# Low parts of weights, masked queries and branch additions move from GpSimd to VectorE, and the planner lets the two engines exclude each other

## The chip, the cores and the metric

The kernel runs on one core of a Trainium2 chip. The core has five engines that run side by side, each with its own queue and its instructions in a fixed order: TensorE (in the profile PE for matmuls, PEld for the loading of weights), VectorE (DVE), ScalarE (ACT), GpSimd (POOL) and SyncE (SP), which issues most transfers. An engine stops at an instruction whose inputs are not there, and everything behind it in its queue stops too. The metric is the device time of one execution in microseconds (us); lower is better.

## What is computed

A batch of one, 512 tokens, 1024 features, all in float32. The first block has two layers. A layer normalizes the tokens (with 16 meta tokens in front, 528 in all), projects them with one wide matrix, runs four token mixers beside each other (A: attention in a window, B: attention with rotary positions, C: differential attention, D: a gated linear recurrence in both directions), gates and adds their results, and ends with a feed-forward network:

```python
for l in range(DEPTH):                                   # 2
    u = rms_norm(h, ln_mix[l])
    (aq, ak, av, bq, bk, bv, cq, ck, cv, dq, dzf, dzb, di, dg, gz) = split_in(u @ w_in[l])
    ...
    gate = jax.nn.sigmoid(gz).reshape(Bn, L, N_BRANCH, D_MODEL)
    merged = gate[:, :, 0] * (y_a @ w_branch[l, 0])
    for n, y in enumerate((y_b, y_c, y_d), start=1):
        merged = merged + gate[:, :, n] * (y @ w_branch[l, n])
    h = h + merged @ w_out[l]
    u = rms_norm(h, ln_ffn[l])
    h = h + (jax.nn.silu(u @ w_ffn_gate[l]) * (u @ w_ffn_up[l])) @ w_ffn_down[l]
```

The second block is one layer: a feed-forward network, a mixer (window attention beside an S5 state-space model) and a second feed-forward network, each with a norm before and after and with shifts and gains from a conditioning vector.

## The kernel before, in words

*Products in three parts.* Every large product runs as three fast matmuls (`mm3`, L258 to L260): a weight `w` and an activation `x` are each split into a high part, which the fast format holds exactly, and a low part, the rest, and high x high, low x high and high x low are added up in PSUM. So each piece of weight that comes from memory (`wload`, L191) goes through two engines: ScalarE copies it into the high part (L218), and a second engine subtracts that from the raw piece to get the low part (L219, pieces of 128x512, some of 128x256). Which engine does it says the list `lo_engs`: the weights of a list of two alternate between its engines. It is VectorE alone at the start, in the output projection (L1696) and in the gate and up projections of the first block's feed-forward networks; it is GpSimd and VectorE by turns in the token mixing of each layer (L1669) and from the start of a layer's down projection (L2186) on, which in the second layer holds for the whole second block. Activations are split likewise (`split`, L230 and L231), with their own choice of engine.

*Token mixing.* A layer first weaves the projections with branches A, B and C; then comes a stage with branch D (`branch_D`, four heads, `d_head`) woven with the merges of branches 1, 2 and 0, and behind it the merge of branch 3. For each head, D goes through levels of 32, 16, 8, 4, 2 and 1 tokens (L1407). A level takes a difference of running sums `d` (L1414, VectorE), its exponentials (L1416 and L1417, ScalarE), the keys times them `kt` (L1419, VectorE), and for levels of 16 and under the queries masked to one half of each block (`masked_q`, L1487, GpSimd), times the exponentials `qm` (L1434, VectorE). Then 16 small matmuls make the level's products on the diagonal blocks (L1403), and VectorE puts them in place by a mask (L1439). Per layer there are 4 x 5 = 20 masked queries.

*Merging.* For a branch `n` and each of eight blocks of features (`merge`, L1492) the kernel makes the gate from the wide projection (24 matmuls per half, tanh on ScalarE, L1514), multiplies it on VectorE with the branch's projection (12 matmuls, L1518), and from the second branch on adds that to the sum (L1520, GpSimd). Layer 0 does so in two halves of 272 and 256 columns, layer 1 in one of 512.

*Order.* Nothing of this is the order on the chip. The whole program is recorded, and then a planner (`Plan`, L2616) simulates it: each instruction has a price by its engine and size (`price`, L2797), there are prices for the signal from one engine to another, and a priority from the length of the work that hangs on it. At each step the engine that is free first takes the ready instruction of the highest priority (`run`, L2875). The order that comes out is written down as the order of every engine's queue, SP's with its transfers too. In the plan, VectorE and GpSimd don't know of each other: a VectorE instruction that is no copy costs 68 + n/0.96 ns for n columns, one of GpSimd 150 + 2.1 n, and after each the engine is free again 60 ns later. Between small matmuls that lie beside each other in the array there is a lower price (`beside`, L2767), and the shape in which the array is used costs nothing to change.

Of the kernel before, what the change touches and what calls it, by code (L numbers as in the profile page):

```python
# [17 lines left out]
ALU = mybir.AluOpType  # L18
PSUM = bass.MemoryType.PSUM
# [100 lines left out]
class Net:  # L120
# [1360 lines left out]
    def masked_q(self, q, m, c0, pool):  # L1481
        qm = self.act_tile(pool, "qm", 3)
        n2 = 2 * m
        o, w = self.offs["qmask"]
        mk = self.misc[:, o + QOFF[m]:o + QOFF[m] + n2]
        nb = (NT - c0) // n2
        self.nc.gpsimd.tensor_tensor(out=qm[:, c0:].rearrange("p (i s) -> p i s", s=n2), in0=q[:, c0:].rearrange("p (i s) -> p i s", s=n2),  # L1487
                                     in1=mk[:, None, :].to_broadcast([P, nb, n2]), op=ALU.mult)
        return qm


    def merge(self, l, n, y, merged, c0, first, pool):  # L1492
# [10 lines left out]
        for f in range(KC):  # L1503
# [13 lines left out]
            def ev2(ps, a, b):  # L1517
                V.scalar_tensor_tensor(out=(m if first else gt)[:, a:b], in0=gt[:, a:b], scalar=1.0, in1=ps, op0=ALU.add, op1=ALU.mult)  # L1518
                if not first:
                    nc.gpsimd.tensor_tensor(out=m[:, a:b], in0=m[:, a:b], in1=gt[:, a:b], op=ALU.add)  # L1520
# [119 lines left out]
    def block1(self, taps=None):  # L1640
        nc = self.nc
        taps = taps or {}
        for l in range(2):
# [10 lines left out]
            with self.pool(f"mix{l}") as mix:  # L1654
# [13 lines left out]
                with self.pool(f"att{l}", "R") as att, self.psum(mm="m"):  # L1668
                    self.lo_engs = [nc.gpsimd, nc.vector]  # L1669
# [141 lines left out]
class Net2(Net):  # L1811
# [368 lines left out]
    def hooks(self, l):  # L2180
# [3 lines left out]
        def down(f):  # L2184
            if f == 0:
                self.lo_engs = [self.nc.gpsimd, self.nc.vector]  # L2186
                if l == 0:
                    self.prep, self.late = self.ssm_prep(), []
                self.prep_on = True
# [426 lines left out]
class Plan:  # L2616
# [8 lines left out]
    TABLE_LOAD, QUEUE, LANES, LANE, DMA_END, DMA_START, WINDOW, WARM = 1283, 32, 8, 900, 940, 650, 3413, 3060  # L2625
# [53 lines left out]
    def trace(self):  # L2679
# [83 lines left out]
        for n, i in enumerate(self.ins):  # L2763
            if self.eng[n] == 0:
                place = self.columns_of(i)
                if place and last and place[0] == last[0] and not place[1] & last[1]:
                    self.beside[n] = last[2], int(2 + 51 * place[2] / 64) + 0  # L2767
# [6 lines left out]
    def written(self):  # L2774
        if not hasattr(self, "_written"):
            self._written = {x.bass_ap.tensor.name for i in self.nc.cur_bb.bb.instructions for x in i.outs if hasattr(x, "bass_ap")}
        return self._written

# [18 lines left out]
    def price(self, i, e, dma, aps):  # L2797
# [7 lines left out]
        if e == 0:  # L2805
# [4 lines left out]
            if mv.dtype == mybir.dt.float32r:  # L2810
                k = 4 if n < 256 else 1
                return int(max(n, m) * k / 2.4) + 3, n * k, 0
# [4 lines left out]
            return int(max(n, m) * 4 / 2.4) + 4, int(4 * n * part), 0  # L2817
# [57 lines left out]
    def run(self):  # L2875
        N = len(self.ins)
        self.columns, self.taken = defaultdict(float), {}
# [8 lines left out]
        free = [0] * 5  # L2886
        lanes, hw, bus, table = [], 0, 0, 0
# [41 lines left out]
        while count < total:  # L2929
# [48 lines left out]
            elif e == 0:  # L2978
                b = self.beside[n]
                c = (b[1] if b and b[0] == before else c[0]), c[1]  # L2980
                self.taken[n] = c[0]
                free[e] = end[n] = self.product(s, *c)
                before, follow = n, self.next.get(n)
            else:
# [4 lines left out]
                end[n] = s + c[0]  # L2989
# [60 lines left out]
```

## Time and profile before

| | us |
|---|---|
| median of three runs | 3429.25 |
| the runs | 3427.11, 3429.25, 3450.57 |
| the profiled execution | 3435.91 |
| its span, first to last instruction | 3434.0 |
| TensorE's mean granted clock in it | 0.939 of full |

The rows below come from the profiled execution. Times in the views count from the start of the span. "Busy" of TensorE counts time in which at least one matmul is under way; a row of matmuls gives each one's own duration, and these overlap. A wait row names the engine and line that waited, then the engine and line that released it, and the idle time, the number of waits and the longest. A stretch of the program stands at: 445 to 695 us branch D with merges in layer 0, 1490 to 1760 the same in layer 1, 150 to 445 and 1250 to 1490 the attention branches, 2150 to 2260 the down projection of layer 1 with the preparation of the S5 model beside it, 3060 to 3350 the last feed-forward network.

### The profile page before, as it was taken

Reading aid. Unit: us, or ns where it says so; the run is one execution under the profiler, and the core shown is the slowest. Engines: PE = TensorE matmul, PEld = TensorE weight load, DVE = VectorE, ACT = ScalarE, POOL = GpSimd, SP = SyncE. Lnnn points to the kernel's source line nnn. Section 1 sums busy time; section 2 is a strip of 40 time slices with the busy share of each in tenths; the row PEclk is TensorE's granted clock in tenths of the full one; section 3 lists DMA queues with packets and bytes.
Section 4 is the critical chain, followed back from the end, with each engine's and each line's share of the span. In section 5 each row is a group of like instructions: output and inputs, shape, how many; then the busy total and the mean of one; then the engine's idle time right before and its main releaser. Section 6 shows DMA issues by size and latency. Waiting matters only on the chain. (4 is left out here: it accounts for less than half of the span.)

```text
span 3434.0 us, 57894 instructions
## 1 busy us (share of the span) xinstructions
PE 3178.3 (93%) x21892; PEld 2775.5 (81%) x21892; DVE 1800.9 (52%) x4554; ACT 1278.3 (37%) x2856; POOL 1070.3 (31%) x952
## 2 busy tenths in 40 slices
PE   7888998999999988998889999999999999989997
PEld 6766877889999976876568888689888888888887
DVE  4556568745644957476875464754111633741113
ACT  2445443334232245653423322234333423542332
POOL 1212244432112331244452111653333411323333
PEclk9988999999999999999999999999999985989998
DMA  5621222344444672122234454474334542333343
GB/s 148 163 49 37 78 59 80 85 123 124 142 121 124 164 170 63 33 85 87 61 98 128 117 163 139 152 217 123 94 95 120 159 150 80 93 102 95 92 120 97
DMA packets 645885, 380.42 MB, mean 111 GB/s; under 512 B 66501, under 2 KB 613885, under 8 KB 645477
## 3 DMA queue, kind: packets, MB, share of 16 engines
q1 hardware_dynamic: 628520, 365.22, 36.5%
q0 software_dynamic: 13632, 9.61, 1.6%
q8 instruction: 172, 2.82, 0.3%
q10 hardware_dynamic: 3452, 1.89, 0.2%
q14 instruction: 109, 0.89, 0.1%
HBM read 333.16 MB, written 45.52 MB: 110 GB/s over the span
## 5 line engine op out<-in xcount | busy, mean ns | idle before, releaser
L258 PE MATMUL ps_mm<-u,wh 128*128 128x256 f32 (+2 forms) x2928 | 972.8, 333 | 38.6 <-ACT g L1514 10.1
L260 PE MATMUL ps_mm<-u,wh 128*128 128x256 f32 (+2 forms) x2928 | 962.5, 330 | 3.1 <-DVE u L231 3.1
L259 PE MATMUL ps_mm<-u,wh 128*128 128x256 f32 (+2 forms) x2912 | 956.2, 329 | 3.6 <-DVE wh L219 2.3
L258 PEld LDWEIGHTS ps_mm<-u,wh 128*128 128x128 f32 x2928 | 563.3, 193 | 100.7 <-ACT g L1514 13.2
L219 POOL TENSOR_TENSOR wh<-wr,wh 128x512 fp32r<-128x512 f32 (+1 forms) x280 | 374.1, 1349 | 764.0 <-ACT wh L218 542.6
L218 ACT ACTIVATE wh<-wr 128x512 fp32r<-128x512 f32 (+1 forms) x588 | 354.7, 618 | 686.5 <-PE ps_mm L260 285.9
L260 PEld LDWEIGHTS ps_mm<-u,wh 128*128 128x128 f32 x2928 | 561.8, 192 | 54.0 <-issue 4.5
L259 PEld LDWEIGHTS ps_mm<-u,wh 128*128 128x128 f32 x2912 | 559.9, 193 | 51.3 <-issue 3.4
L219 DVE TENSOR_TENSOR wh<-wr,wh 128x512 fp32r<-128x512 f32 (+1 forms) x251 | 184.5, 749 | 395.8 <-issue 120.2
L259 PE MATMUL ps_mm<-hid,wh 128*128 128x256 f32 (+2 forms) x988 | 301.9, 311 | 3.5 <-DVE wh L219 2.7
L258 PE MATMUL ps_mm<-hid,wh 128*128 128x256 f32 (+2 forms) x948 | 291.1, 313 | 0.0
L260 PE MATMUL ps_mm<-hid,wh 128*128 128x256 f32 (+2 forms) x948 | 290.9, 312 | 0.0
L231 POOL TENSOR_TENSOR hid<-g,hid 128x512 fp32r<-128x512 f32 (+1 forms) x85 | 93.1, 1096 | 518.5 <-ACT hid L230 513.4
L1846 DVE SCALAR_TENSOR_TENSOR acc<-ho,cact,acc 128x128 f32<-128x128 f32 x504 | 217.9, 438 | 27.6 <-DMA ho<-in_w_ada_dram 18.3
L259 PEld LDWEIGHTS ps_mm<-hid,wh 128*128 128x128 f32 x988 | 186.8, 191 | 14.8 <-DVE wh L219 3.6
L260 PEld LDWEIGHTS ps_mm<-hid,wh 128*128 128x128 f32 x948 | 179.4, 192 | 10.4 <-issue 0.8
L258 PEld LDWEIGHTS ps_mm<-hid,wh 128*128 128x128 f32 x948 | 179.5, 192 | 10.1 <-issue 0.4
L218 ACT ACTIVATE wh<-wrx 128x512 fp32r<-128x512 f32 (+1 forms) x160 | 96.1, 601 | 209.6 <-PE ps_mm L260 126.9
L258 PE MATMUL ps_mm<-u,hid 128*128 128x256 f32 (+1 forms) x448 | 136.7, 305 | 16.7 <-ACT hid L218 16.7
L259 PE MATMUL ps_mm<-u,hid 128*128 128x256 f32 (+1 forms) x448 | 136.4, 305 | 6.8 <-DVE hid L219 6.8
L219 DVE TENSOR_TENSOR wh<-wrx,wh 128x512 fp32r<-128x512 f32 x83 | 58.1, 700 | 150.8 <-issue 68.6
L260 PE MATMUL ps_mm<-u,hid 128*128 128x256 f32 (+1 forms) x448 | 134.8, 301 | 0.0
(599 smaller groups left out, 6152.2 us busy)
## 6 DMA issues: line engine op xcount, KB each, us to landing
wr<-in_w_in_dram SPq DMA_DIRECT2D x220, 256.0 KB
ho<-in_w_ada_dram SPq DMA_DIRECT2D x144, 256.0 KB
wr<-in_w_ffn_down_dram SPq DMA_DIRECT2D x80, 256.0 KB
wr<-in_w_down_dram SPq DMA_DIRECT2D x66, 256.0 KB
wr<-in_w_ffn_gate_dram SPq DMA_DIRECT2D x62, 256.0 KB
wr<-in_w_gate_dram SPq DMA_DIRECT2D x61, 256.0 KB
wr<-in_w_ffn_up_dram SPq DMA_DIRECT2D x60, 256.0 KB
wr<-in_w_up_dram SPq DMA_DIRECT2D x60, 256.0 KB
```

Source lines behind the costliest of these rows:

```text
L218: self.last_split = nc.scalar.activation(hi[:, i:e], raw, AF.Copy)
L219: (nc.vector if o else eng).tensor_tensor(out=lo[:, i:e], in0=raw, in1=hi[:, i:e].bitcast(F32), op=ALU.subtract)
L231: (eng or self.nc.vector).tensor_tensor(out=lo, in0=x, in1=hi.bitcast(F32), op=ALU.subtract)
L258: T.matmul(o, lhsT=wh, rhs=xh[:, a:b], start=start, stop=False)
L259: T.matmul(o, lhsT=wl, rhs=xh[:, a:b], start=False, stop=False)
L260: T.matmul(o, lhsT=wh, rhs=xl[:, a:b], start=False, stop=stop)
L1846: V.scalar_tensor_tensor(out=acc, in0=w[:, k], scalar=c, in1=acc, op0=ALU.mult, op1=ALU.add)
```

## The change

Four edits move work, and the rest changes the planner. All low parts are made on VectorE; the masked query of D and the addition of a branch go to VectorE as well. What stays on GpSimd: the low parts of activations that `split` gives it, the sums of squares, the copies into `U` at the start of a head of D, a few products of the S5 preparation and its DMA issues.

```diff
     def masked_q(self, q, m, c0, pool):
...
-        self.nc.gpsimd.tensor_tensor(out=qm[:, c0:].rearrange("p (i s) -> p i s", s=n2), in0=q[:, c0:].rearrange("p (i s) -> p i s", s=n2),
+        self.nc.vector.tensor_tensor(out=qm[:, c0:].rearrange("p (i s) -> p i s", s=n2), in0=q[:, c0:].rearrange("p (i s) -> p i s", s=n2),
...
                 if not first:
-                    nc.gpsimd.tensor_tensor(out=m[:, a:b], in0=m[:, a:b], in1=gt[:, a:b], op=ALU.add)
+                    V.tensor_tensor(out=m[:, a:b], in0=m[:, a:b], in1=gt[:, a:b], op=ALU.add)
...
                 with self.pool(f"att{l}", "R") as att, self.psum(mm="m"):
-                    self.lo_engs = [nc.gpsimd, nc.vector]
+                    self.lo_engs = [nc.vector]
...
         def down(f):
             if f == 0:
-                self.lo_engs = [self.nc.gpsimd, self.nc.vector]
+                self.lo_engs = [self.nc.vector]
```

In the planner, a VectorE instruction (engine 2 in the code) whose inputs all lie in SBUF, and a GpSimd instruction (engine 3) with more than one input, take a common "port": each begins when the port is free and holds it to its end. A change of the shape in which TensorE's array is used costs 95 or 190 ns, and some prices of matmuls change.

```diff
+    def shares(self, n, e):
+        if n not in self.sources:
+            aps = [x.bass_ap for x in self.ins[n].ins if getattr(x, "bass_ap", None) is not None]
+            psum = any(str(x.tensor.space).endswith("PSUM") for x in aps)
+            self.sources[n] = not psum and (e == 2 or e == 3 and len(aps) > 1)
+        return self.sources[n]
...
-                    self.beside[n] = last[2], int(2 + 51 * place[2] / 64) + 0
+                    self.beside[n] = last[2], int(2 + 8 * place[2] / 64)
...
-                k = 4 if n < 256 else 1
-                return int(max(n, m) * k / 2.4) + 3, n * k, 0
+                if n < 256:
+                    return max(105, int(n * 4 / 2.4)), n * 4, 0
+                return int(n * 0.449 + 3.5), n, 0
...
-            return int(max(n, m) * 4 / 2.4) + 4, int(4 * n * part), 0
+            return int(max(n, m) * 4 / 2.4) + 9, int(4 * n * part), 0
...
+                new = self.layout_of(n) or shape
+                if new != shape:
+                    c = c[0] + (self.REGROUP if new[0] == shape[0] else 2 * self.REGROUP), c[1]
+                    shape = new
...
-                end[n] = s + c[0]
+                begin = s
+                if self.shares(n, e):
+                    begin = max(s, port)
+                    port = begin + c[0]
+                end[n] = begin + c[0]
                 free[e] = end[n] + (20 if e == 1 else 60)
```

So the order of every engine is computed anew. VectorE in branch D of layer 0, head 0, levels 8 and 4, before (`d_`, `kt_` and `qm_` are a level's difference, keys and queries, `wb_` a low part, `hn_` the sum of branches):

```order
L1419 TENSOR_TENSOR kt_959_4719<-kk0_1573,d_958_4715 128x528
L1434 TENSOR_TENSOR qm_960_4721<-qm_960_4721,d_958_4715 128x528
L1518 SCALAR_TENSOR_TENSOR hn_1046_5228<-g_1047_5229,ps_mm_1051_5290 128x256
L1419 TENSOR_TENSOR kt_980_4850<-kk0_1573,d_979_4846 128x528
L1439 COPY_PREDICATED D_937_4573<-mask_484,ps_d_961_4724 128x128
L1434 TENSOR_TENSOR qm_981_4852<-qm_981_4852,d_979_4846 128x528
L219 TENSOR_TENSOR wb_1110_5645<-wr_1111_5646,wb_1110_5645 128x256
```

VectorE at the same place now (`wh_` is a low part of a weight of the wide projection):

```order
L1487 TENSOR_TENSOR qm_960_4721<-qq0_3992,misc_72 128x528
L1419 TENSOR_TENSOR kt_959_4719<-kk0_1573,d_958_4715 128x528
L1434 TENSOR_TENSOR qm_960_4721<-qm_960_4721,d_958_4715 128x528
L1487 TENSOR_TENSOR qm_981_4852<-qq0_3992,misc_72 128x528
L1414 TENSOR_TENSOR d_984_4876<-U_884_4294,lf0_3141 128x528
L219 TENSOR_TENSOR wb_1089_5499<-wr_1090_5500,wb_1089_5499 128x256
L1414 TENSOR_TENSOR d_1001_4991<-U_884_4294,lf0_3141 128x528
L219 TENSOR_TENSOR wh_1092_5505<-wr_1094_5510,wh_1091_5504 128x512
L1487 TENSOR_TENSOR qm_986_4882<-qq0_3992,misc_72 128x528
L1419 TENSOR_TENSOR kt_980_4850<-kk0_1573,d_979_4846 128x528
L1434 TENSOR_TENSOR qm_981_4852<-qm_981_4852,d_979_4846 128x528
```

Between two levels' queries (`qm_960` and `qm_981`) VectorE had three instructions, and now has seven: two masked queries, two low parts, two differences and the next keys.

GpSimd at that place, before:

```order
L219 TENSOR_TENSOR wh_1092_5505<-wr_1094_5510,wh_1091_5504 128x512
L1487 TENSOR_TENSOR qm_956_4694<-qq0_3992,misc_72 128x512
L1487 TENSOR_TENSOR qm_960_4721<-qq0_3992,misc_72 128x528
L219 TENSOR_TENSOR wh_1113_5651<-wr_1114_5652,wh_1112_5650 128x512
L1487 TENSOR_TENSOR qm_981_4852<-qq0_3992,misc_72 128x528
L1487 TENSOR_TENSOR qm_986_4882<-qq0_3992,misc_72 128x528
```

And now, where only the copies into `U` at the start of each head are left:

```order
L1309 COPY U_884_4294<-lf0_3141 64x528
L1315 COPY U_884_4294<-lf0_3141 64x8x63
L1313 MEMSET U_884_4294 64x8
L1314 COPY U_884_4294<-lf0_3141 64x15
L1310 MEMSET U_884_4294 64x1
L1309 COPY U_1028_5169<-lf0_3141 64x528
```

VectorE in the attention stretch of layer 1, at the first maxima of branch C (`ISA` on L1096), before:

```order
L219 TENSOR_TENSOR wh_2509_15243<-wr_2511_15248,wh_2508_15242 128x512
L1096 ISA g_2442_15010,tmC_2439_15007<-ps_s_2443_15011,tab_2437_15004 128x264
L1096 ISA tmC_2439_15007 128x1
L1096 ISA g_2442_15010,ngC_2440_15008<-ps_s_2444_15014,tab_2437_15004,tmC_2439_15007 128x264
L1096 ISA ngC_2440_15008 128x1
```

And now:

```order
L219 TENSOR_TENSOR wh_2509_15243<-wr_2511_15248,wh_2508_15242 128x512
L1096 ISA g_2442_15010,tmC_2439_15007<-ps_s_2443_15011,tab_2437_15004 128x264
L1096 ISA tmC_2439_15007 128x1
L219 TENSOR_TENSOR wh_2536_15354<-wr_2537_15355,wh_2535_15353 128x512
L1096 ISA g_2442_15010,ngC_2440_15008<-ps_s_2444_15014,tab_2437_15004,tmC_2439_15007 128x264
```

A low part that GpSimd made before stands between the two halves of a score row.

## Rows read from the trace of the kernel before

**Rows 1.** The page: busy us, share of the span and instructions by engine
```profile
PE 3178.3 (93%) x21892; PEld 2775.5 (81%) x21892; DVE 1800.9 (52%) x4554; ACT 1278.3 (37%) x2856; POOL 1070.3 (31%) x952
```
**Rows 2.** Stretches: start:end length, busy of PE, PEld, DVE, ACT, POOL, PEclk, DMA, GB/s
```profile
445.00:695.00 250.00, 228.86 (x2413) 198.11 (x2413) 195.94 (x381) 93.64 (x241) 120.16 (x103) 0.92 0.27 77
...
1250.00:1490.00 240.00, 213.66 (x1635) 176.00 (x1635) 144.35 (x591) 139.84 (x328) 51.99 (x45) 0.93 0.28 64
1490.00:1760.00 270.00, 234.52 (x1898) 171.24 (x1897) 206.53 (x329) 104.54 (x254) 127.65 (x102) 0.93 0.28 80
...
2150.00:2260.00 110.00, 103.19 (x548) 77.56 (x547) 85.68 (x111) 25.11 (x46) 77.09 (x49) 0.97 0.53 166
...
3060.00:3350.00 290.00, 290.00 (x1423) 242.85 (x1423) 45.98 (x75) 86.97 (x160) 95.45 (x79) 1.00 0.34 99
```
**Rows 3.** Waits of PE, first three from 450 to 700 us, then from 1500 to 1760
```profile
PE ps_mm L258 <- ACT g L1514: 8.4, 6, 3.7
PE ps_d L1403 <- DVE qm L1434: 7.1, 5, 2.6
PE ps_mm L258 <- DVE g L1518: 4.0, 3, 2.3
...
PE ps_mm L258 <- DVE hn L1518: 6.8, 3, 5.0
PE ps_mm L258 <- ACT g L1514: 6.6, 8, 2.0
PE ps_d L1403 <- DVE qm L1434: 5.7, 5, 2.3
PE ps_d L1463 <- DVE AO L1455: 4.0, 1, 4.0
PE ps_mm L258 <- DVE g L1518: 3.7, 3, 2.0
```
**Rows 4.** Timeline 511 to 516 us, start and length: GpSimd, VectorE, then TensorE
```profile
511.24 2.98 POOL L1487 TENSOR_TENSOR qm<-qq,misc 128x528 f32<-128x528 f32 x2
...
511.63 1.41 DVE L1419 TENSOR_TENSOR kt<-kk,d 128x528 f32<-128x528 f32 x1
512.97 1.81 DVE L1434 TENSOR_TENSOR qm<-qm,d 128x528 f32<-128x528 f32 x1
514.71 0.70 DVE L1419 TENSOR_TENSOR kt<-kk,d 128x528 f32<-128x528 f32 x1
...
514.84 0.46 PE L1403 MATMUL ps_d<-qm,kt 128*32 128x32 f32 x32 [1.76 <-DVE qm L1434]
```
**Rows 5.** Lines: busy us and mean ns, or duration ns min/median/max
```profile
L1434 DVE TENSOR_TENSOR qm<-qm,d 128x528 f32<-128x528 f32 (+1 forms) x40 | 48.9, 1223 | 0.0
L1419 DVE TENSOR_TENSOR kt<-kk,d 128x528 f32<-128x528 f32 (+1 forms) x48 | 56.5, 1177 | 19.0 <-PE ps_d L1380 9.0 <-PE ps_d L1391 4.5 <-PE ps_d L1427 2.7
...
L1434 DVE TENSOR_TENSOR qm<-qm,d x40: 677/1135/1943, 447.9 to 1735.9; 128x528 f32<-128x528 f32 x32, 128x512 f32<-128x512 f32 x8
...
L219 DVE TENSOR_TENSOR hid<-wr,hid x33: 676/680/1229, 809.0 to 3053.4; 128x512 fp32r<-128x512 f32 x33
...
L231 DVE TENSOR_TENSOR u<-g,u x56: 408/428/1506, 30.2 to 3055.9; 128x256 fp32r<-128x256 f32 x44, 128x272 fp32r<-128x272 f32 x12
```
**Rows 6.** Stretches, GpSimd's instructions of L219 alone: busy us and count, PEclk, DMA, GB/s
```profile
150.00:445.00 295.00, 39.23 (x30) 0.91 0.21 54
445.00:695.00 250.00, 54.33 (x40) 0.92 0.27 77
...
1250.00:1490.00 240.00, 24.47 (x19) 0.93 0.28 64
1490.00:1760.00 270.00, 69.12 (x49) 0.93 0.28 80
```
**Rows 7.** Waits of PE from 1250 to 1500 us
```profile
PE ps_s L1095 <- DVE tmC L1096: 10.4, 3, 4.8
```

More of the change, by code (lines that the diff above doesn't have):

```diff
@@ L2624 @@
     TABLES = {"Exp": 1, "Tanh": 1, "Sigmoid": 2, "Ln": 3, "Silu": 4}
-    TABLE_LOAD, QUEUE, LANES, LANE, DMA_END, DMA_START, WINDOW, WARM = 1283, 32, 8, 900, 940, 650, 3413, 3060
+    TABLE_LOAD, QUEUE, LANES, LANE, DMA_END, DMA_START, WINDOW, WARM, REGROUP = 1283, 32, 8, 900, 940, 650, 3413, 3060, 95
     def __init__(self, tc, slack):
@@ L2777, in written, with layout_of @@
         return self._written
+    def shares(self, n, e):
[4 more added lines that the diff above has]
+        return self.sources[n]
+    def layout_of(self, n):
+        if n not in self.layouts:
+            i = self.ins[n]
+            wt = i.ins[1].bass_ap if i.opcode == "Matmult" else None
+            self.layouts[n] = None if wt is None else tuple(next(s for s in (32, 64, 128) if x <= s) for x in (wt.ap[0][1], self.free(wt)))
+        return self.layouts[n]
     @staticmethod
@@ L2876, in run @@
         N = len(self.ins)
-        self.columns, self.taken = defaultdict(float), {}
+        self.columns, self.taken, self.layouts, self.sources, shape = defaultdict(float), {}, {}, {}, (P, P)
         tail = self.tails()
@@ L2886, in run @@
         free = [0] * 5
+        port = 0
         lanes, hw, bus, table = [], 0, 0, 0
```

## The prediction

> **What bounds the kernel now.** I read the busy shares first: TensorE has work in flight for 93% of the span, VectorE for 52%, GpSimd for 31% [rows 1]. So a VectorE instruction that gets cheaper gains nothing by itself; only time in which TensorE stands still, or runs at the lower of its two clock levels (granted 0.5, that is 1.2 instead of 2.4 GHz), can be given back. Second, the table by stretches says where that time lies [rows 2]. In the feed-forward stretch 3060 to 3350, TensorE is busy 290.0 of 290 us at a granted clock of 1.00: nothing that the change does there can show. In the two stretches of branch D with the gated merges beside it (445 to 695 in layer 0, 1490 to 1760 in layer 1) it is busy 228.9 of 250 and 234.5 of 270 us, at 0.92 and 0.93. That is 21.1 + 35.5 = 56.6 us of pauses. A mean of 0.92 over two levels means 0.08 x 250 x 2 = 40 us at the lower one, 0.93 over 270 us means 38 us; each such microsecond does half the work, so 20 + 19 = 39 us are lost there too. These 96 us are what the change can reach, and both stretches have a VectorE at 78% and 76% (195.9 and 206.5 us) with GpSimd at 48% (120.2, 127.7) beside it.
>
> Third, the waits of TensorE in these two stretches [rows 3] (read from 450 and from 1500 us on). VectorE's rows (L1434, L1518, L1455) are 7.1 + 4.0 = 11.1 us in layer 0 and 6.8 + 5.7 + 4.0 + 3.7 = 20.2 us in layer 1, 31.3 together; ScalarE's gate (L1514) holds 8.4 + 6.6 = 15.0; the rest, 10.3, is in small rows. Fourth, the timeline shows what makes VectorE late [rows 4]. GpSimd runs two masked queries (L1487) from 511.24 for 2.98 us. VectorE's L1434 beside them takes 1.81 us from 512.97, and the instructions just behind, when GpSimd is through, take 0.70. TensorE waits 1.76 us for that L1434. By the per-line rows [rows 5] L1434 takes 677 ns at best and 1223 in the mean, L1419, which has the same shape and kind, 1177. Of the 48.9 + 56.5 = 105.4 us of these two lines, (40 + 48) x 0.677 = 59.6 are work and 45.8 (43%) are standing beside GpSimd.
>
> The Trainium skill has a rule for this: "SBUF — State Buffer", section "SBUF: two separate sides", says that a VectorE instruction with two SBUF inputs and a GpSimd one that reads SBUF exclude each other for the whole instruction. The rows at 511 to 515 us agree, with 1.81 against 0.70 us. By the rule alone all lengthening in the two stretches would end, and VectorE would come out at the lower end of the load given below; it also works against the change, since the GpSimd work that stays is then locked out by 508 more instructions of VectorE.
>
> **The change, part by part.** Counted in the two programs, GpSimd goes from 957 instructions to 449 and VectorE from 4556 to 5064: 508 move, 40 masked queries, 72 additions of branches, and 396 low parts. TensorE, ScalarE and SP have the same number as before, so no transfer is added; GpSimd's own DMA issues have less ahead of them.
>
> *Price on VectorE.* A low part of 128x512 takes 0.68 us there undisturbed (median of the 33 on L219 for the tile hid), one of 256 columns 0.41 (the smallest of L231) [rows 5]. A masked query has the shape of L1419 and L1434: the trace has none on VectorE, so it costs between 0.68 (L1434's best) and 1.18 (L1419's mean beside GpSimd); I take 0.68, since the GpSimd that lengthens it is what leaves. An addition costs 0.41 or 0.68 by its width. In branch D's stretches 40 + 49 = 89 low parts move [rows 6], with the 40 masked queries and the additions of two of the three later branches, 32 of half width in layer 0 and 16 of 512 columns in layer 1: 89 x 0.68 + 40 x 0.68 + 32 x 0.41 + 16 x 0.68 = 61 + 27 + 13 + 11 = 112 us more. Against that, at least the 45.8 us of the two lines go. If the other two-input instructions there (some 250 us of VectorE's busy time in all, an estimate from the 402.4 less what reads PSUM or is tiny) lose 43% likewise, it is 107. So VectorE's load goes from 402.4 to between 407 and 469 of 520 us, from 77% to between 78% and 90%. It does not get freer. I take the lower half, 420, because the rows at 511 to 515 return to 0.70 as soon as GpSimd is idle.
>
> *What gets earlier.* The gain is not in load but in two other places. A diagonal level no longer waits for an instruction of 1.6 us on a second engine, and the one that ends last (L1434) comes at its 0.68. And the order of all engines is written by a planner that priced these instructions at 68 + 528/0.96 = 618 ns, with 60 more before the next, and had no notion that two engines exclude each other: its TensorE order put D's matmuls where an L1434 of 0.68 us would have been done, and the chip delivered it after 1.22. Now the planner makes one engine wait for the other, and almost nothing is left to wait for in D (the copies into U alone stay on GpSimd). So TensorE's order fits what VectorE delivers. I let three quarters of VectorE's 31.3 us go (-23), a third of the 25.3 us behind the gate and in the small rows (-8), since the gate's bank is released by L1518 in the same VectorE queue, and, with the pauses, a third of the 39 us lost to the low clock level (-13): -44. Bounds: 0, if the fuller queue is as late as the slow one was, and -86 (nine tenths of 96).
>
> *Elsewhere.* In 2150 to 2260 (the S5 preparation beside the down projection) GpSimd is busy 77.1 us and VectorE 85.7 of 110, TensorE pauses 6.8 [rows 2]. The low parts leave GpSimd, the preparation's own products stay: -3, bounds 0 and -7. In the attention stretch of layer 1 (1250 to 1490) GpSimd is busy 52.0 of 240 us, VectorE 144.4, and TensorE waits 10.4 us for VectorE's maximum of branch C [rows 2, 7]. There the low parts get into the one queue that also has the softmax; the order shows one between two score instructions. Each one that stands in front of a chain costs up to 0.68; 30 + 19 = 49 come into the two attention stretches [rows 6] and I let one in eight count: +4, bounds 0 and 49 x 0.68 = +33. At the boundaries between the second block's stages, where TensorE pauses too and low parts move as well, the same by estimate: +3, bounds -5 and +20. The last edit, the planner's prices of matmuls and of a change of array shape, only reorders: 763 changes of shape stand in TensorE's order before and 772 now, so it removes none. I take 0, with 20 us to both sides, a tenth of the 199 us of pauses outside branch D.
>
> Sum against the profiled execution (3435.9 us, of which 3434.0 are the span and 1.9 lie around it): -44 - 3 + 4 + 3 = -40, 3396. The median of the runs shown is 6.7 lower, 3429.25, so 3389 in its terms.
>
> **Rivals.**
>
> *VectorE stays as late as it was.* For it: its load doesn't fall (78 to 90% against 77%), and in D it is a serial chain with the queue of the low parts now in it. Against it: rows 4 show the wait to be exclusion, not load. Then only -3, +4 and +3 remain and a few microseconds of pauses: 3420 to 3435, taken as 3428.
>
> *TensorE becomes the bound of branch D too.* If the order fits everywhere, four fifths of the 56.6 us of pauses (45) and three quarters of the 39 (29) go: -74, with the other terms 3359. For it: the saturated stretch in rows 2 shows that this engine runs without a pause when its inputs are ahead. Against it: the gate's 15.0 us hang on PSUM banks, which the change doesn't touch.
>
> *Slower: one queue for everything.* VectorE in D ends near 90%, and a low part, whose matmuls come later, stands before a mask or a product that TensorE needs now. VectorE's waits there (31.3 us) then double, and the attention stretches pay the half of their bound: +31 + 17 = +48, 3477; with half of each, 3453. It decides from a load of about 460 us of 520 in the two stretches on, that is if less than 53 us of the lengthening goes.
>
> **How the numbers follow.** Forecast 0.48, around 3389, own range 3365 to 3413; VectorE as late as before 0.23; TensorE as bound 0.13; slower 0.16. A difference of 1% (34 us, 3395 and 3463 being the borders) is about what a measurement of this kernel tells from none. Faster by over 1%: 0.64 of the forecast's cases (0.31), all of the third (0.13) and a little of the others: 0.45. Within 1%: the rest of the forecast and nearly all of the second, 0.17 + 0.21, and of the slower case those that stop short of 3463, 0.03: 0.41. Slower: 0.14. The range 3335 to 3445 leaves out the worst part of the slower case and the extreme of the third, with 20 us for the reordering in both ends.
>
> **What would show it right or wrong.** Right: L1434 and L1419 near 0.69 us in the mean, GpSimd almost idle in branch D, VectorE's busy time there between 400 and 440 us, TensorE's waits for L1434 and L1518 under half of 31.3 us, and D's two stretches shorter by some 20 us each; L1487 at about 0.69 on VectorE. Wrong: the durations fall as said but D's stretches stay as long (the chain, not the exclusion, was the limit); or attention and the stage boundaries lengthen by more than 10 us; or the time moves in a stretch where TensorE was saturated, which only the reordering or the clock could do.

## The result, and the profile after

The changed kernel takes 3330.66 us (median of 4 runs, 3323.5 to 3333.74) against 3438.98 us of the kernel before, timed beside it (4 runs, 3427.11 to 3450.57): ratio 0.9682, 95% interval 0.9637 to 0.9728. Against these four runs it is faster by 108 us; against the 3429.25 us from which the forecast was counted, by 98.6, where 40 were forecast. The time lies just under the low end of the range (3335).

The page, busy times by engine, answers to [rows 1]:

```profile
PE 3146.6 (94%) x21892; PEld 2761.1 (83%) x21892; DVE 1856.6 (56%) x5062; ACT 1278.9 (38%) x2856; POOL 416.9 (13%) x444
```

To find where the time went I cut both profiled executions at the same instructions: the first level difference of branch D (L1414), the first addition of the output projection (L1544) and the first instruction of the second block (L2238), as each layer has them.

| stage | before, us | after, us | difference |
|---|---|---|---|
| start and attention of layer 0 | 398.3 | 389.8 | -8.5 |
| branch D and merges, layer 0 | 360.2 | 319.3 | -40.9 |
| feed-forward of layer 0, attention of layer 1 | 751.6 | 757.2 | +5.6 |
| branch D and merges, layer 1 | 333.4 | 283.2 | -50.2 |
| feed-forward, layer 1 | 448.2 | 440.8 | -7.4 |
| second block | 1142.3 | 1141.7 | -0.6 |
| span | 3434.0 | 3332.0 | -102.0 |

So 91.1 of the 102 us come from the two stages of branch D. They are longer than the two stretches of [rows 2], which lay inside them but for 20 us at the start of the second; here are the whole stages in the table by stretches (start:end, length, busy of PE, PEld, DVE, ACT, POOL, granted clock, DMA share, GB/s), first of the kernel before:

```profile
398.30:758.50 360.20, 331.23 (x3204) 295.44 (x3203) 242.40 (x464) 129.03 (x321) 157.87 (x136) 0.94 0.28 82
1510.10:1843.50 333.40, 293.67 (x2111) 216.23 (x2110) 242.59 (x391) 120.85 (x281) 152.74 (x112) 0.94 0.31 89
```

and of the changed kernel:

```profile
389.80:709.10 319.30, 317.16 (x3195) 285.02 (x3194) 232.12 (x579) 127.53 (x316) 5.10 (x10) 0.99 0.31 88
1466.30:1749.50 283.20, 276.85 (x2109) 206.94 (x2108) 222.59 (x491) 121.54 (x282) 4.60 (x10) 1.00 0.36 103
```

The reader is to see four things. TensorE's pauses (length less busy) go from 29.0 + 39.7 = 68.7 us to 2.1 + 6.4 = 8.5: 60.2 us. Its busy time goes from 624.9 to 594.0 for the same matmuls, 30.9 us, while the granted clock rises from 0.94 to 0.99 and 1.00: by these rounded means about 83 us were spent at 1.2 GHz and now 6, an estimate that makes 38 us of gain. The pauses and the busy time together are the 91.1 us. GpSimd falls from 310.6 us to 9.7. And VectorE, which takes over 200-odd instructions there (855 before, 1070 now), is busy for less time than before: 454.7 instead of 485.0 us.

The waits of TensorE in the two stages, layer 0 and then layer 1, answer to [rows 3]; the long waits are gone, none is over 0.9 us:

```profile
PE ps_mm L260 <- DVE msp L231: 0.9, 1, 0.9
PE ps_mm L258 <- DVE g L1518: 0.6, 2, 0.4
PE ps_d L1380 <- ACT AO L1373: 0.2, 1, 0.2
```

```profile
PE ps_mm L258 <- ACT g L1514: 5.0, 9, 0.9
PE ps_d L1380 <- ACT AO L1373: 0.7, 2, 0.5
PE ps_t L1848 <- DVE acc L1846: 0.3, 1, 0.3
```

The lines of VectorE (busy us, mean ns) answer to [rows 5]. L1434 falls from 1223 to 693 ns, L1419 from 1177 to 694; the moved masked query takes 708. The last line, L1846, makes the running sums of the second block's modulation, which the planner spreads over these and other stages:

```profile
L1520 DVE TENSOR_TENSOR hn<-hn,g 128x272 f32<-128x272 f32 (+1 forms) x72 | 35.9, 510 | 0.1
L1419 DVE TENSOR_TENSOR kt<-kk,d 128x528 f32<-128x528 f32 (+1 forms) x48 | 33.3, 694 | 3.5 <-PE ps_d L1380 1.8 <-PE ps_d L1427 0.8 <-PE ps_d L1391 0.6
L1487 DVE TENSOR_TENSOR qm<-qq,misc 128x528 f32<-128x528 f32 (+1 forms) x40 | 28.3, 708 | 3.5 <-PE ps_d L1391 1.8 <-PE ps_d L1403 1.7
L1434 DVE TENSOR_TENSOR qm<-qm,d 128x528 f32<-128x528 f32 (+1 forms) x40 | 27.7, 693 | 0.0
L1846 DVE SCALAR_TENSOR_TENSOR acc<-ho,cact,acc 128x128 f32<-128x128 f32 x504 | 186.4, 373 | 37.7 <-DMA ho<-in_w_ada_dram 30.1
```

Before, L1846 and the difference L1414 (694 ns now) stood at:

```profile
L1414 DVE TENSOR_TENSOR d<-U,lf 128x528 f32<-128x528 f32 (+1 forms) x48 | 44.1, 927 | 0.9 <-PE ps_d L1472 0.9
L1846 DVE SCALAR_TENSOR_TENSOR acc<-ho,cact,acc 128x128 f32<-128x128 f32 x504 | 217.9, 438 | 27.6 <-DMA ho<-in_w_ada_dram 18.3
```

The timeline of VectorE at a level of layer 0 (start, length) answers to [rows 4]: the two products of the level stand side by side at 0.69, and the low parts (L219) fill in behind them:

```profile
544.04 0.69 DVE L1419 TENSOR_TENSOR kt<-kk,d 128x528 f32<-128x528 f32 x1
544.66 0.69 DVE L1434 TENSOR_TENSOR qm<-qm,d 128x528 f32<-128x528 f32 x1
...
547.53 0.67 DVE L219 TENSOR_TENSOR wh<-wr,wh 128x512 fp32r<-128x512 f32 x1
...
549.15 0.67 DVE L219 TENSOR_TENSOR wh<-wr,wh 128x512 fp32r<-128x512 f32 x1
```

### The profile page after: what moved, and what is told of

Read it like the earlier page. It is cut to its first block, busy times and chain, and to the rows that moved or that the text cites. A ratio compares the mean times of both kernels' runs of the same rounds, so it can differ in the third digit from the quotient of the medians.

```text
span 3332.0 us, 57805 instructions
## 1 busy us (share of the span) xinstructions
PE 3146.6 (94%) x21892; PEld 2761.1 (83%) x21892; DVE 1856.6 (56%) x5062; ACT 1278.9 (38%) x2856; POOL 416.9 (13%) x444
## 5 line engine op out<-in xcount | busy, mean ns | idle before, releaser
L219 DVE TENSOR_TENSOR wh<-wr,wh 128x512 fp32r<-128x512 f32 (+1 forms) x531 | 367.3, 703 | 460.3 <-issue 228.1
L259 PE MATMUL ps_mm<-hid,wh 128*128 128x256 f32 (+2 forms) x988 | 298.3, 310 | 3.2 <-DVE wh L219 3.1
L258 PE MATMUL ps_mm<-hid,wh 128*128 128x256 f32 (+2 forms) x948 | 287.4, 312 | 2.8 <-ACT wh L218 2.8
L260 PE MATMUL ps_mm<-hid,wh 128*128 128x256 f32 (+2 forms) x948 | 287.1, 311 | 0.0
L1846 DVE SCALAR_TENSOR_TENSOR acc<-ho,cact,acc 128x128 f32<-128x128 f32 x504 | 186.4, 373 | 37.7 <-DMA ho<-in_w_ada_dram 30.1
L219 DVE TENSOR_TENSOR wh<-wrx,wh 128x512 fp32r<-128x512 f32 (+1 forms) x131 | 87.4, 667 | 136.7 <-issue 116.4
L88 POOL TENSOR_TENSOR na<-na,g 128x256 f32<-128x256 f32 (+2 forms) x62 | 63.1, 1018 | 778.8 <-issue 418.1
```

The source lines that it names most:

```text
L88: nc.gpsimd.tensor_tensor(out=acc[:, a:b], in0=acc[:, a:b], in1=sq[:, a:b], op=ALU.add)
L219: (nc.vector if o else eng).tensor_tensor(out=lo[:, i:e], in0=raw, in1=hi[:, i:e].bitcast(F32), op=ALU.subtract)
L258: T.matmul(o, lhsT=wh, rhs=xh[:, a:b], start=start, stop=False)
L259: T.matmul(o, lhsT=wl, rhs=xh[:, a:b], start=False, stop=False)
L260: T.matmul(o, lhsT=wh, rhs=xl[:, a:b], start=False, stop=stop)
L1846: V.scalar_tensor_tensor(out=acc, in0=w[:, k], scalar=c, in1=acc, op0=ALU.mult, op1=ALU.add)
```

## The experiments

All were timed beside the kernel before, each pair on one chip, but e1 to e7, e8 to e10, e11 and e12, and e13 and e14 on four different ones; ratios are against it. "D" is the sum of the two stages of branch D in the one profiled execution (before 693.6, changed kernel 602.5 us). Three executions in which D has nearly the same order (changed kernel, e3, e10) give 602.5, 601.9 and 602.6 us for it. Whole kernels differ by more, by the clock of the second block above all (last section). Where an edit changes the work in D, the planner lays its order anew, so such a run differs from the changed kernel by its order as well.

**Are the moves the cause, or the planner?** The change moves work and also teaches the planner new rules. Each half alone:

```
e1: the four edits of lines 1487 to 2186 as changed; class Plan as before
e2: these four edits undone; class Plan as changed
e3: the changed kernel, without the planner's turn-taking:
-                if self.shares(n, e):
+                if False:
e4: the changed kernel, with the old matmul prices, no price for a
    change of array shape, and beside[n] at 51 instead of 8 per 64
```

Moves only. 

> The four moves to VectorE with the planner of before (no common port, old prices of matmuls). Theory A, exclusion: GpSimd's work beside VectorE was what made VectorE late, so the moves alone give 70 to 100 of the 108 us (3340 to 3370), L1434 near 0.69 us, pauses of TensorE in the two stretches of branch D under 25 us. Theory B, the planner: what gave the gain is an order that fits, and the moves alone give at most 40 us (3400 or more), with pauses in D above 40 us.

Planner only. 

> The planner of the changed kernel (common port, shape changes, new matmul prices) with the work left on GpSimd. Theory A: 0 to 25 us faster than before, and L1434 and L1419 in the mean still above 0.9 us, since the exclusion itself stays. Theory B: 60 us or more.

No turn-taking. 

> The changed kernel, the planner without the common port but with its other new prices. Theory A: after the moves almost no GpSimd work is left in branch D, so the port matters little there: within 10 us of the changed kernel, the difference outside D. Theory B with the port as its cause: 40 us or more slower than the changed kernel.

Turn-taking with the old prices. 

> The changed kernel with the common port, but the planner's old prices of matmuls, of neighbours in the array and of shape changes. Theory A: within 10 us of the changed kernel. Theory B with the matmul prices as its cause: 40 us or more slower than the changed kernel.

| kernel | median us | ratio, 95% interval | D, us | pauses in D | L1434, ns |
|---|---|---|---|---|---|
| e1 moves only | 3351.85 | 0.9754 (0.9730 to 0.9778) | 607.0 | 17.3 | 695 |
| e2 planner only | 3387.69 | 0.9867 (0.9839 to 0.9895) | 649.4 | 42.2 | 1227 |
| e3 no turn-taking | 3346.81 | 0.9746 (0.9717 to 0.9774) | 601.9 | 8.5 | 695 |
| e4 old prices | 3327.00 | 0.9688 (0.9614 to 0.9761) | 607.4 | 17.1 | 696 |

The moves alone shorten D by 86.6 of the 91.1 us, and the whole by 84 of the 108 us, as theory A expected of e1. The planner alone gives 44.2 us in D without making L1434 any shorter. By median it gives 48 us in all: more than the 0 to 25 that theory A gave it, less than the 60 of theory B. I read this as an order that puts other work in front of what will be late; no run has the turn-taking alone with the work left on GpSimd, so which of the planner's rules did it stays open. 86.6 and 44.2 are more than the 91.1 of both: they are in part substitutes. Once the work has moved, the turn-taking has nothing left to do in D: without it D has nearly the same order and length (601.9 against 602.5). The new prices do a little there: with the old ones the pauses in D are 17 us instead of 8.5, and D is about 5 us longer, with turn-taking (e4) and without (e1).

Outside D both of the planner's parts matter, the turn-taking and the new prices. The start takes 377.5 to 392.6 us in the nine kernels that have both (changed kernel, e2, e8 to e14), and 396.1 to 402.8 in the seven that lack one or both (before, e1, e3 to e7). So the 8.5 us won at the start go to the planner and not to the moves. Their size is uncertain: nearly the same order of the start takes 377.5 to 392.6 us in single executions. e3 is 16 us slower than the changed kernel by median, where theory A allowed 10, and e1 is 21 us slower. e4's median looks level with it, but two of its four runs (3304 and 3305 us) had a mean granted clock of 0.961. The other two (3349 and 3352, at 0.948) are some 20 us slower than the changed kernel at 0.948 to 0.954. By them the new prices are worth about as much as the turn-taking; on two runs that is a hint.

**Which move?** One at a time, with the planner as before:

```
e5:  -  self.lo_engs = [nc.gpsimd, nc.vector]      (and L2186)
     +  self.lo_engs = [nc.vector]
e6:  -  self.nc.gpsimd.tensor_tensor(out=qm[:, c0:]...
     +  self.nc.vector.tensor_tensor(out=qm[:, c0:]...
e7:  -  nc.gpsimd.tensor_tensor(out=m[:, a:b]...
     +  V.tensor_tensor(out=m[:, a:b]...
```

Low parts. 

> Only the low parts go to VectorE (both places), planner as before. All four moves together, with the planner as before, took 84 us off. Exclusion theory (what counts is how long GpSimd reads SBUF beside branch D): the low parts are 160.9 of GpSimd's 310.6 us in the two stages of branch D, so about half of the gain, -43 us (-35 to -55), and L1434 falls about half way, to 0.90-1.05 us. Chain rival (what counts is that the masked query, a step of the chain itself, sits on a slow second engine): the low parts are off the chain, so -15 us or less.

Masked queries. 

> Only the masked queries go to VectorE, planner as before. Exclusion theory: they are about 60 of the 310.6 us of GpSimd in the two stages of branch D, so a fifth of the gain of all moves, -16 us (-8 to -25), L1434 still above 1.0 us. Chain rival: -40 us or more, most of what all moves give, since each diagonal level gets rid of a step of 1.5 us and of two hand-overs between engines.

Additions. 

> Only the additions of branches go to VectorE, planner as before. Exclusion theory: 79.5 of the 310.6 us of GpSimd in the two stages, so a quarter of the gain, -21 us (-12 to -30), L1434 at 1.0-1.15. Chain rival: nothing, -3 to +3, since no other instruction of the stage waits for them soon.

| kernel | median us | ratio, 95% interval | D, us | GpSimd busy in D | L1434, ns |
|---|---|---|---|---|---|
| e5 low parts | 3324.18 | 0.9713 (0.9651 to 0.9775) | 624.1 | 156.1 | 1069 |
| e6 masked queries | 3395.50 | 0.9904 (0.9883 to 0.9925) | 644.9 | 254.6 | 902 |
| e7 additions | 3418.31 | 0.9953 (0.9936 to 0.9970) | 667.3 | 232.0 | 1121 |

In D that is -69.5, -48.7 and -26.3, together 144.5 against 86.6 for all at once: each takes away waits that another would also have taken away. Only the additions came out as the exclusion theory expected (-15 us in all, L1434 at 1121 ns), and against the chain rival, which gave them nothing. The low parts gave more than expected (-69.5 in D, where -35 to -55 was set), with L1434 a little above its bounds (1069 ns against 1050). The masked queries missed it clearly: with 63.6 of GpSimd's 310.6 us they bring -38 us in all (-8 to -25 expected, -40 or more by the chain rival) and more than half of the gain in D. L1434 falls furthest with them. They stand in the very place of the timeline where the products of the level stand [rows 4], so I take it that beside what GpSimd works counts more than how long. That fits the chain rival as well, so the next runs had to part them. (e5's total of -109 us has 44 from the second block, which has nothing to do with the stage; see the last section.)

**Exclusion or a shorter chain?** The changed kernel with all moves made, and GpSimd given work again that nobody waits for, in every level:

```
             qt = self.masked_q(q, m, c0, pool)
+            idle = pool.tile([P, 192], F32, tag="idle", ...)
+            nc.gpsimd.tensor_copy(out=idle[:, :8], in_=e[:, NM:NM + 8])
e8:  +       6 x nc.gpsimd.tensor_tensor(out=idle, in0=q[:, NM:NM + 192],
                                         in1=q[:, NM + 192:NM + 384], op=ALU.mult)
e9:  +       14 x nc.gpsimd.memset(idle, 0.0)
e11: +       10 x nc.gpsimd.tensor_copy(out=idle, in_=q[:, NM:NM + 192])
```

Idle products. 

> The changed kernel, and GpSimd gets work again that nobody needs: beside each masked query a small copy that waits for the level's exponentials, and six products of two SBUF pieces of 192 columns into a scratch tile that nobody reads. No step of branch D waits for it. The changed kernel stood at ratio 0.968 of the kernel before, L1434 at 0.69 us. Exclusion theory: VectorE's two-input instructions get long again though every move stays made: L1434 and L1419 together above 0.95 us in the mean, the two stages of branch D 30 us or more longer than the changed kernel's 602.5, ratio 0.976 to 0.990. Rival (what helped was the shorter chain and fewer hand-overs): L1434 at most 0.75, ratio 0.964 to 0.973.

Idle memsets. 

> As the kernel with idle products, but GpSimd only writes: fourteen memsets of the same scratch tile in place of the six products, about the same busy time on GpSimd. If the exclusion needs GpSimd to read SBUF, nothing happens: L1434 at 0.69 to 0.75 us, ratio 0.964 to 0.973. If any work of GpSimd on SBUF holds VectorE up, it comes out like the kernel with idle products: L1434 above 0.9, ratio 0.976 or more.

Idle copies. 

> As the kernel with idle products (ratio 0.984) and the one with idle memsets (0.9705), but GpSimd's idle work is ten copies of one SBUF piece of 192 columns beside each masked query. If one SBUF input is enough to hold VectorE up: L1434 and L1419 at 0.80 us or more, ratio 0.976 or more. If it takes two: 0.69 to 0.73 us, ratio 0.966 to 0.973.

The idle work in the per-line view of GpSimd, of e8, e9 and e11 in turn:

```profile
L1437 POOL TENSOR_TENSOR idle<-qq 128x192 f32<-128x192 f32 x240 | 207.8, 866 | 18.9
```

```profile
L1437 POOL MEMSET idle<- 128x192 f32 x560 | 144.7, 258 | 32.3
```

```profile
L1437 POOL COPY idle<-qq 128x192 f32<-128x192 f32 x400 | 232.9, 582 | 24.4
```

| kernel | median us | ratio, 95% interval | D, us | VectorE busy in D | L1434 (L1438 there), ns |
|---|---|---|---|---|---|
| e8 products | 3377.76 | 0.9836 (0.9807 to 0.9865) | 646.6 | 508.1 | 903 |
| e9 memsets | 3333.43 | 0.9705 (0.9686 to 0.9724) | 607.1 | 455.8 | 714 |
| e11 copies | 3343.84 | 0.9715 (0.9690 to 0.9739) | 610.7 | 482.0 | 786 |

e8 decides that the exclusion is real and costs time. Every step of the chain is on VectorE as in the changed kernel, nobody waits for the idle products, and VectorE is busy 53.4 us longer for the same number of instructions; D is 44.1 us longer, and TensorE waits for L1434's product again (5.9 us in layer 0, 4.8 in layer 1):

```profile
PE ps_d L1403 <- DVE qm L1438: 5.9, 3, 4.7
...
PE ps_d L1403 <- DVE qm L1438: 4.8, 3, 2.7
```

L1434 and L1419 (824 ns) came out a little under the 0.95 I had set, the time as expected. It does not decide that the exclusion was the whole gain: GpSimd gets back 227.6 of the 300.9 us that it lost in D, and D gets back 44.1 of 91.1. Whether a chain with fewer hand-overs has a part in the rest, and how much of the 44.1 is the hold-up itself and how much the order that the planner laid around the idle work, no run separates. The lines of VectorE in e8 show who is held up and who isn't:

```profile
L1419 DVE TENSOR_TENSOR kt<-kk,d 128x528 f32<-128x528 f32 (+1 forms) x48 | 39.5, 824 | 6.4 <-ACT d L1417 5.6 <-PE ps_d L1403 0.4 <-PE ps_d L1391 0.3
L1522 DVE SCALAR_TENSOR_TENSOR g<-g,ps_mm 128x272 f32<-128x272 f32 (+1 forms) x72 | 36.2, 508 | 17.7 <-PE ps_mm L260 8.6 <-ACT g L1518 8.4 <-ACT wh L218 0.3
L1438 DVE TENSOR_TENSOR qm<-qm,d 128x528 f32<-128x528 f32 (+1 forms) x40 | 36.1, 903 | 0.0
L1459 DVE COPY AO<-D 32x128 f32<-32x128 f32 x16 | 6.6, 414 | 0.3
```

The merge's L1518 (L1522 there), which reads one operand from PSUM, takes 508 ns as in the changed kernel. Memsets, which read nothing, hold up next to nothing (714 against 693 ns, VectorE 1.1 us longer in D); they came to 144.7 us of GpSimd instead of about the 207.8 of the products, too small a difference to explain 1.1 against 53.4. Copies with one input lie between, and neither expectation for them held: L1434 at 786 ns, above the 730 of the one and under the 800 of the other, and 233 us of them lengthen VectorE by 27.3 us and D by 8.2.

**Is VectorE's load the limit?** If standing beside GpSimd costs time, does VectorE's own work cost as much? The changed kernel with idle products on VectorE, in the levels (e12 five each, e14 two) or beside the merge (e13):

```
e12: +       5 x V.tensor_tensor(out=idle, in0=q[:, NM:NM + 192], in1=e[:, NM:NM + 192], ...)
e14: +       2 x the same            (both right behind the masked query)
e13: +       3 x V.tensor_tensor(out=idle, in0=m[:, a:a + 192], in1=m[:, a:a + 192], ...)
             (behind each L1520)
```

Five per level. 

> The changed kernel, and VectorE itself gets idle work beside each masked query: five products of two SBUF pieces of 192 columns into a scratch tile that nobody reads, 200 instructions of about 0.27 us, 54 us in the two stages of branch D; GpSimd stays idle. It is worked out to VectorE's load of before the change and somewhat above (about 510 of 602 us). Exclusion theory (VectorE's load has slack, only being held up inside a chain cost time): 0 to 15 us against the changed kernel, ratio 0.968 to 0.974. Rival (VectorE's load decides, whatever it consists of): TensorE's pauses in branch D come back, 25 us or more, ratio 0.976 or more.

Beside the merge. 

> The changed kernel, and VectorE gets idle work off the chain of branch D: three products of 192 columns into a scratch tile that nobody reads behind each addition of branches, 216 instructions, about 78 us at the 0.361 us that such a product took inside the levels, all in the two stages of branch D. Theory now (the chain of a diagonal level decides; what the order can put into VectorE's gaps is nearly free): at most 15 us against the changed kernel, ratio 0.968 to 0.974. Rival (VectorE's load decides, wherever it stands): as with the idle products in the levels, 35 us or more, ratio 0.979 or more.

Two per level. 

> As the kernel with five idle products of VectorE in each diagonal level (72 us of them, ratio 0.9805), but two: 29 us. Theory now (each level is a chain, so each microsecond in it counts from the first on, at 43/72 = 0.6): +17 us against the changed kernel, ratio 0.973 to 0.977. Rival (there is a load from which it costs): 0 to 5 us, ratio 0.968 to 0.9715.

| kernel | idle work, us | median us | ratio, 95% interval | D, us | longer than 602.5 by | per us of idle work |
|---|---|---|---|---|---|---|
| e12 | 72.2 | 3374.20 | 0.9805 (0.9777 to 0.9832) | 648.4 | 45.9 | 0.64 |
| e14 | 28.6 | 3341.38 | 0.9734 (0.9700 to 0.9768) | 621.6 | 19.1 | 0.67 |
| e13 | 76.9 | 3350.15 | 0.9759 (0.9727 to 0.9791) | 621.3 | 18.8 | 0.24 |

e12 went against the theory that VectorE's load has slack: it expected 0 to 15 us. Inside a diagonal level each microsecond of idle work on VectorE costs about 0.65 us of D, from the first 29 us on (e14, as expected; its ratio alone can't be told from the changed kernel's, since the intervals overlap). Beside the merge the same work costs a little over a third of that. It is not free, as I had it (at most 15 us), nor does load alone decide. For standing beside GpSimd the price is not one number: e8 pays 44.1 us for 53.4 that VectorE is longer busy (0.83), e11 8.2 for 27.3 (0.30). TensorE's pauses tell e12 and e13 apart as well: 40.7 us in e12, 16.7 in e13, with VectorE busy 519 and 521 us in the two. The waits of TensorE in e12, layer 1, show the place, the product L1434 (L1437 there):

```profile
PE ps_d L1403 <- DVE qm L1437: 11.7, 7, 3.4
PE ps_mm L258 <- ACT g L1517: 8.1, 13, 0.9
```

**Further in the same direction.** Three more lines of two-operand instructions go from GpSimd to VectorE:

```
L985:  - nc.gpsimd.tensor_tensor(      + V.tensor_tensor(
L675:  - (nc.gpsimd if s else nc.vector).tensor_tensor(   + nc.vector.tensor_tensor(
L2118: - G.tensor_tensor(              + self.nc.vector.tensor_tensor(
```

> The changed kernel, and three more products and differences of two SBUF operands go from GpSimd to VectorE: the rotation's product (L985, 6 of 1.34 us), the low part of the second half of a query (L675, 4 of 1.5 us) and the products of the S5 preparation (L2118, 24 of 1.70 us). Exclusion theory: where TensorE is saturated nothing is gained; the two in the attention stages stand on a chain that TensorE waits for in part, so -2 to -10 us against the changed kernel, ratio 0.965 to 0.968. Rival (VectorE's queue fills up in the preparation): +5 us or more in the stage of the second feed-forward part, ratio 0.970 or more.

3335.43 us, ratio 0.9715 (0.9690 to 0.9739), inside the interval of the changed kernel. D is untouched (602.6), the second feed-forward stage 445.8 against 440.8 us, the attention 764.3 against 757.2. The expected -2 to -10 us did not come; ratio and stage are what the rival set (0.970, +5 us), but other kernels with the moves take 439.0 to 445.2 us for that stage, so the rival isn't shown either. Nothing beats the changed kernel for certain. The medians of e4 (3327.0) and e5 (3324.2) are lower, but their intervals hold its ratio, and their profiled executions have it from the clock of the second block (last section).

## Why the prediction was wrong in size and right in kind

*What bounds it:* right. The two stages of branch D gave 91 of 102 us; the saturated stretches gave nothing, and in the second block 210 us less of GpSimd's work (366 to 156) left the length as it was.

*The mechanism, exclusion between GpSimd and VectorE:* right as far as it goes, shown by e8 against e9; that it is the whole of the gain is not shown. L1434 and L1419 came out at 0.69 as said, L1487 at 0.71, GpSimd almost idle.

*Where the 62 us between -40 and -102 lie.* By the stages of e1, in single executions, the moves alone gave -86.6 in D and +2.3 outside it, and the planner's new rules -17.7 on top. The forecast had -44, +4 and 0.

*The step that failed* is in "What gets earlier": "I let three quarters of VectorE's 31.3 us go (-23), a third of the 25.3 us behind the gate and in the small rows (-8) [...] a third of the 39 us lost to the low clock level (-13): -44". Of what the whole stages offered (68.7 us of pauses, and 0.06 x 693.6 = 41.6 lost to the clock) 60.2 (88%) and 30.9 (74%) went, where I had let 55% of the pauses and a third of the clock go. Together that is 83%, near my outer bound of nine tenths. Shares by releaser were the wrong unit. The gate's row, for which I let a third go, went from these two lines, of layer 0 and layer 1 in whole stages,

```profile
PE ps_mm L258 <- ACT g L1514: 8.9, 9, 3.7
...
PE ps_mm L258 <- ACT g L1514: 10.8, 13, 2.0
```

to none and 5.0 us. I read that as one origin for most rows, an order that fell behind VectorE; no run shows the origin of a single pause, and in layer 1 much of the gate's row stays with the moves alone (8.1 us in e1). The clock rose as the pauses fell, 0.94 to 0.99 and 1.00, so the second term should have gone with the first. The tie is loose: e6 is granted 1.00 in layer 1 with 27.6 us of pauses, e13 0.96 in layer 0 with 8.2.

*The load term under it* also failed: "from 402.4 to between 407 and 469 [...]. It does not get freer." I took 420, that is +4%; in the whole stages VectorE's busy time fell by 6%, from 485.0 to 454.7. By the durations of its instructions there, form by form, about 142 us came (113 low parts 78, masked queries 28, additions 36) and about 148 went in instructions that were there before. The rest of the fall is that the records of neighbouring instructions overlap more, by 68 us instead of 46, and that nine instructions of L1846 stand elsewhere. My 46 to 107 were for three quarters of that length; scaled to the whole that is 61 to 143, so slightly more went than my upper end. Of the 148, 56 are L1434, L1419 and L1414, 32 the running sums L1846 (505 to 348 ns in these stages), 18 the low parts that VectorE made before. So well under half of it lay in the products of the diagonal levels.

*Half of its reason* was not borne out either: "Now the planner makes one engine wait for the other". In D that rule does nothing once the moves are made (e3).

*Elsewhere:* with the moves alone (e1) the start, feed-forward and attention came to +7.6 us where I had +4 for attention, the stage with the S5 preparation to -4.5 (-3), the second block to -0.8 (+3): all within what single executions of these stages differ by. The last edit's prices, put at 0 with 20 to both sides, are worth some 5 us in D.

*Rivals.* "VectorE stays as late as it was" fell with TensorE's waits. "TensorE becomes the bound of branch D too" is what happened: busy 594.0 of 602.5 us. I gave it 3359 and 0.13, because I took the gate's 15 us as hanging on PSUM banks; the measured time lies another 28 us below it. "One queue for everything" is a real force (e12, e13: 0.64 and 0.24 per us), yet the 142 us that came were no more than the 148 that went.

## What to carry to other kernels

When two engines exclude each other, price a move by what stands beside the instruction in the timeline, and by all two-operand lines of the stage, not by the moved instruction or by one line's mean. If the waits in a stage seem to have one origin, take as forecast that all rows go together, those under other engines' names and the lost clock included, and keep partial shares for the range. Price a new order by itself too. Work put on the receiving engine still costs: put it off the chain (0.24 us per us here), not in it (0.65).

## What the runs showed of the hardware

VectorE's copy AO<-D (L1455), with one SBUF input and no second one, takes 221 ns in the changed kernel and 414 beside e8's products, 246 beside e9's memsets; L1434, with two inputs, takes 903 beside the products and 714 beside the memsets. The copy in the changed kernel, 390 to 716 us, by line:

```profile
L1455 DVE COPY AO<-D 32x128 f32<-32x128 f32 x8 | 1.8, 221 | 0.2
```

The Trainium skill ("SBUF — State Buffer", "SBUF: two separate sides") puts VectorE's two-port modes under the same lock as its instructions with two SBUF inputs, and wants GpSimd to read SBUF for the latter. On the latter the runs agree; that this copy runs in such a mode no run shows. Unexpected was the difference between GpSimd's forms: 208 us of products held VectorE up for 53.4 us, 233 us of copies for 27.3, less than half per microsecond, and D grew by 44.1 against 8.2. No run settles why.

The clock made a difference of some 43 us that no edit made. In the mixer of the second block the changed kernel's TensorE is busy without a pause and is still granted 0.50, its lower level, for about 100 us:

```profile
2680.00:2700.00 20.00, 19.96 (x113) 16.69 (x112) 6.85 (x31) 2.93 (x4) 0.00 (x0) 0.97 0.58 187
2700.00:2720.00 20.00, 20.00 (x79) 16.74 (x79) 10.00 (x37) 3.99 (x18) 2.53 (x2) 0.50 0.57 181
...
2760.00:2780.00 20.00, 20.00 (x92) 19.02 (x92) 4.16 (x11) 9.21 (x27) 1.46 (x2) 0.50 0.35 117
```

while e5, with the same instructions there in a slightly other order, keeps 1.00 and has a second block of 1098.3 instead of 1141.7 us:

```profile
2694.00:2714.00 20.00, 20.00 (x160) 19.46 (x159) 2.37 (x5) 4.71 (x10) 3.69 (x4) 1.00 0.69 210
2714.00:2734.00 20.00, 20.00 (x107) 16.40 (x105) 3.52 (x11) 4.01 (x6) 0.00 (x0) 1.00 0.36 116
2734.00:2754.00 20.00, 18.87 (x136) 15.53 (x135) 15.88 (x65) 4.58 (x21) 2.53 (x2) 1.00 0.89 282
```

The order alone does not decide it. e1 and e5 run the second block in the same order on TensorE, VectorE, ScalarE and GpSimd, operation by operation and tile by tile in the traces, and still differ; the stage in e1 and in e5:

```profile
2208.20:3349.70 1141.50, 1084.11 (x6154) 958.84 (x6152) 457.29 (x1058) 410.14 (x871) 160.04 (x157) 0.91 0.38 112
...
2223.80:3322.10 1098.30, 1043.44 (x6155) 923.72 (x6153) 456.86 (x1058) 408.91 (x871) 159.50 (x157) 0.95 0.39 117
```

One program does both: e4's four runs took 3304, 3305, 3349 and 3352 us, at a mean granted clock of 0.961, 0.961, 0.948 and 0.948, and the one of them that was profiled (3305) kept 1.00 there. What tips it was not tried.
